# The first norm of a two-layer trunk: the input loaded a second time with tokens on partitions, and four of its products moved to GpSimd

## The chip, the cores and the metric

The kernel runs on one core of one Trainium2 chip. The metric is the device time of one execution in microseconds (us), the median of several runs. A core has five engines with instruction streams of their own: TensorE (PE, whose weight loads are PEld), VectorE (DVE), ScalarE (ACT), GpSimd (POOL) and SyncE (SP, which here only issues transfers). They wait for each other by semaphores. DMA engines move data between the chip's memory and the on-chip buffers. In the profile TensorE's clock is a share of full speed: 1.00 is the 2.4 GHz level, 0.50 the 1.2 GHz level.

## What is computed

The program is a trunk of two layers over 512 tokens of 1024 features, with 256 tokens of context beside them. The layer that the change touches begins with an RMSNorm, is modulated by a conditioning vector `c`, and goes into one wide projection:

```python
def rms_norm(x, w):
    x32 = x.astype(jnp.float32)
    y = x32 * lax.rsqrt(jnp.mean(x32 * x32, axis=-1, keepdims=True) + EPS)
    return (y * w.astype(jnp.float32)).astype(x.dtype)

def modulate(h, shift, scale):
    return h * (1.0 + scale) + shift
```

Shift and scale are products of the activated `c` with a modulation matrix, `ada_w`. The projected columns feed a bidirectional retention (queries, keys, values and a gate g) and a convolution. The retention's decay per head is a fixed function of the eight numbers `ret_decay_logit`. An output projection and a SwiGLU feed-forward follow, then a second layer of another kind.

## The kernel before, in words

Features lie on the 128 partitions. The residual stream is eight tiles `x0` to `x7`, one for each 128 features, of 128 x 512 (512 tokens). Every large product is done with both operands split into a high and a low part: three products (`mm3`, L506) of 128 x 128 by 128 x 512. The high part is a copy on ACT (`hi_of`), the low part a difference on DVE (`lo_of`). Nearly all records of an engine show the line of its helper: MM on PE is L328, DVE's helper is L299, ACT's L313, POOL's L307.

The work around the change is `even_start`. Its stages before the change:

- SP loads the eight tiles of xT (256 KB each), the constants kst, then the rows of `ada_w` (`load_ada`, two of 512 KB for each feature tile) and the rows of the projection's weights (`load_wr`, 512 KB per feature tile).
- ACT squares each tile of x, DVE adds the squares up, and PE multiplies the sum by a column of ones (`p4`), so that four columns of 128 tokens' sums stand on partitions. DVE makes `v` of them, and POOL raises it to the power of -1/2 (`r`). Four diagonal blocks of r (`dg`) times a matrix of ones give `pb`, the norm's factor of every token on all partitions.
- POOL has a chain of small operations before that power: a polynomial in `z` of 128 x 8 for the retention's decay. It ends in `lg`, `nlg`, `lw` and `xb`. All is issued in program order, and each engine works its stream off in order.
- `c_rows` spreads the activated conditioning rows over the partitions with two one-row matmuls for each of two rows (latents and context); ACT puts them into `cbx` and `cbc`. `dots(k, i)` takes the inner products of a tile's rows of `ada_w` with such a row on DVE (128 x 1024, with an accumulator), and `cols(k)` makes of them the columns `acol` and `xacc`.
- The loop over the eight feature tiles k: ACT takes the high parts of the weight rows, DVE runs `dots(k, 1)` and `cols(k)`, then t = x_k * rb (rb is pb copied by ACT), ACT applies scale and shift and takes the high part of t, DVE takes the low parts of the two weight halves, runs `dots(k + 1, 0)` and takes the low part of t. PE does 24 products per tile, into eight banks that stay open over all eight tiles.
- For k above 3 the weights of the queries are also loaded (`q_load`, L910 and L913), in four buffers shared with the weight rows. They are split by `q_split`, four times within the loop (`Q_AT`) and four times behind it: ACT takes the high part and its negative, and a transfer that POOL issues adds the weights to that negative, which leaves the low part (`add_dma`, L332, in the rows `a<-raw`). PE takes the query products up behind the loop. The line L476 in SP's rows loads the weights of g, which come next.

`warm()` issues products of ones that nothing reads. The name `pg` in the rows is any bank, `a` any 128 x 512 slot, `raw` a buffer of weight rows, `ar` one of rows of `ada_w`, `pw` (after the change) the bank of the warm products. What sets the order is the order of the code and, for transfers, the buffers that must be free.

Of the kernel before, what the change touches and what calls it, by code (L numbers as in the profile page):

```python
# [15 lines left out]
P = 128  # L16
D = 1024
# [27 lines left out]
WARM2 = 2  # L45
# [22 lines left out]
LATE_STEP = 2  # L68
COLD = 3.0
# [182 lines left out]
def trunk_kernel(ctx: ExitStack, tc: tile.TileContext, A, out: bass.AP):  # L252
# [94 lines left out]
    nc.scalar.dma_start(out=lgz, in_=A["ret_decay_logit"].partition_broadcast(P))  # L347
    ident = kst[:, K_ID:K_ID + P]
# [7 lines left out]
    ACT(out=first, in_=mhalf, func=AF.Exp)  # L356
    xT = []
    for k in range(KD):
        x = xres.tile([P, T], F32, name=f"x{k}")
        nc.sync.dma_start(out=x, in_=A["xT"][k * P:(k + 1) * P, :])  # L360
        xT.append(x)
    nc.sync.dma_start(out=kst, in_=A["kst"])
# [143 lines left out]
    def mm3(ps, L, R, first, last):  # L506
        (lh, ll), (rh, rl) = L, R
        MM(ps, lh, rl, start=first, stop=False)
        MM(ps, lh, rh, start=False, stop=False)
        MM(ps, ll, rh, start=False, stop=last)  # L510
        tick(3 * rh.shape[1] / 2400)
# [324 lines left out]
    def even_start(pool):  # L836
# [15 lines left out]

        crow = []
# [7 lines left out]
        def load_wr(k):  # L861
            wr = wraw.tile([P, D], F32, name=nm("raw"), tag="raw")
            nc.sync.dma_start(out=wr, in_=w_in[k * P:(k + 1) * P, 2048:3072])
            wrs.append(wr)
# [8 lines left out]
        def warm(n, rhs):  # L873

            ps = bank()
# [44 lines left out]

        raws.append(load_ada(0))
# [9 lines left out]
        sums = []  # L931
        for k in range(KD):
            q = slot()
            ACT(out=q, in_=xT[k], func=AF.Square)
            warm(WARM0, xT[k])
            if len(sums) == 2:
                TT(out=q, in0=sums.pop(0), in1=q, op=ALU.add)
            sums.append(q)
            if k == 0:
                e = pool.tile([P, 8], F32, name="z2")  # L940
                ACT(out=e, in_=z1, func=AF.Exp)
                ACT(out=first, in_=mhalf, func=AF.Silu)
                d2 = pool.tile([P, 8], F32, name="z3")
                GTS(out=d2, in0=e, scalar1=2.0, scalar2=None, op0=ALU.add)
                nc.vector.reciprocal(out=d2, in_=d2)
                sv = pool.tile([P, 8], F32, name="z4")
                GTT(out=sv, in0=e, in1=d2, op=ALU.mult)
                s2 = pool.tile([P, 8], F32, name="z5")
                GTT(out=s2, in0=sv, in1=sv, op=ALU.mult)
# [1174 lines left out]
```

## Time and profile before

| | |
|---|---|
| runs | 1117.42, 1117.03 and 1114.89 us, median 1117.03 us |
| profiled execution | 1115.2 us, of which the span of its engines' work is 1113.4 us |
| mean granted clock of TensorE | 0.991 |
| busy: PE, PEld | 1090.6 us (98%), 961.0 us (86%) |
| busy: DVE, ACT, POOL | 887.7 us (80%), 501.6 us (45%), 121.3 us (11%) |
| chain that ended last, by engine | PE 91%, DMA 2%, DVE 2%, issue 2%, POOL 1%, ACT 1% |

The times within the trace are microseconds from the start of the span. A row of a timeline gives the start, the time from the first start to the last end of neighbouring instructions of one form, the engine, the line, the operation, what it writes and reads, the shapes, the count, and in brackets how long the engine stood idle before and what ended that. SPq and POOLq are transfers being issued, and their landing is told in the DMA views.

### The profile page before, as it was taken

Reading aid. Unit: us, or ns where it says so; the run is one execution under the profiler, and the core shown is the slowest. Engines: PE = TensorE matmul, PEld = TensorE weight load, DVE = VectorE, ACT = ScalarE, POOL = GpSimd, SP = SyncE. Lnnn points to the kernel's source line nnn. Section 1 sums busy time; section 2 is a strip of 40 time slices with the busy share of each in tenths; the row PEclk is TensorE's granted clock in tenths of the full one; section 3 lists DMA queues with packets and bytes.
Section 4 is the critical chain, followed back from the end, with each engine's and each line's share of the span. In section 5 each row is a group of like instructions: output and inputs, shape, how many; then the busy total and the mean of one; then the engine's idle time right before and its main releaser. Section 6 shows DMA issues by size and latency. Waiting matters only on the chain.

```text
span 1113.4 us, 16976 instructions
## 1 busy us (share of the span) xinstructions
PE 1090.6 (98%) x6554; PEld 961.0 (86%) x6554; DVE 887.7 (80%) x1444; ACT 501.6 (45%) x759; POOL 121.3 (11%) x140
## 2 busy tenths in 40 slices
PE   6999999999999999999999999999999999999996
PEld 3878887469988999999999988899889999999996
DVE  5989998998779798788898788776796756667666
ACT  5556756567533344243345443534334442434331
POOL 4022122213000000000001010000001000000000
PEclk7999999999999999999999999999999999999998
DMA  9789976659266688777787335334755676565502
GB/s 352 235 217 263 279 190 162 176 178 232 87 209 196 175 250 244 221 205 225 210 243 196 124 114 189 114 77 137 208 147 139 149 178 161 144 168 136 148 11 76
DMA packets 132224, 199.42 MB, mean 179 GB/s; under 512 B 7088, under 2 KB 91440, under 8 KB 132144
## 3 DMA queue, kind: packets, MB, share of 16 engines
q1 hardware_dynamic: 99392, 137.01, 37.7%
q0 software_dynamic: 24592, 34.85, 19.1%
q10 hardware_dynamic: 8160, 26.48, 7.0%
q8 instruction: 51, 0.84, 0.3%
q14 instruction: 29, 0.24, 0.1%
HBM read 178.16 MB, written 2.10 MB: 162 GB/s over the span
## 4 chain that ended last, share of the span: by engine, by line
PE 91%; DMA 2%; DVE 2%; issue 2%; POOL 1%; ACT 1%; POOLq 0%; DVEq 0%; ACTq 0%
PE pg L328 61%; PE pg L1865 29%; PE pm L328 2%; DVE a L299 2%; DMA wl<-raw 1%; POOL z L307 1%; DMA a<-raw 1%; ACT a L313 1%; DMA x<-in_xT 0%; DMA raw<-in_ffn_w_gate 0%; ACT wh L313 0%; POOL s L307 0%; DVE wl L299 0%; DMA a<-a 0%; ACT dm L313 0%
## 5 line engine op out<-in xcount | busy, mean ns | idle before, releaser
L328 PE MATMUL pg<-a,wh 128*128 128x512 f32 (+1 forms) x1504 | 381.3, 344 | 1.0 <-DVE x L299 0.9
L313 ACT ACTIVATE wh<-raw 128x1024 fp32r<-128x1024 f32 (+1 forms) x219 | 227.2, 1042 | 324.4 <-PE pg L328 137.2
L1865 PE MATMUL pg<-a,wh 128*128 128x256 f32 x1792 | 323.4, 283 | 0.0
L299 DVE TENSOR_TENSOR wl<-raw,wh 128x1024 fp32r<-128x1024 f32 (+1 forms) x203 | 242.9, 1200 | 99.0 <-ACT wh L313 97.6
L328 PEld LDWEIGHTS pg<-a,wh 128*128 128x128 f32 x1504 | 260.4, 190 | 34.8 <-DVE x L299 1.3
L1865 PEld LDWEIGHTS pg<-a,wh 128*128 128x128 f32 x1792 | 281.0, 192 | 1.7
L328 PE MATMUL pg<-a,wl 128*128 128x512 f32 (+1 forms) x752 | 257.5, 343 | 0.0
L1865 PE MATMUL pg<-a,wl 128*128 128x256 f32 x896 | 253.6, 283 | 0.0
L1865 PEld LDWEIGHTS pg<-a,wl 128*128 128x128 f32 x896 | 172.0, 192 | 0.0
L328 PEld LDWEIGHTS pg<-a,wl 128*128 128x128 f32 x752 | 142.5, 190 | 16.8 <-issue 0.5
L328 PE MATMUL pg<-a,a 128*128 128x512 f32 (+2 forms) x572 | 128.1, 379 | 2.2 <-DMA a<-raw 1.5
L299 DVE SCALAR_TENSOR_TENSOR x<-pg,mod,x 128x512 f32<-128x512 f32 (+1 forms) x140 | 85.0, 625 | 47.8 <-PE pg L328 47.1
L328 PEld LDWEIGHTS pg<-a,a 128*128 128x128 f32 x572 | 97.3, 192 | 28.4 <-issue 8.8
L328 PE MATMUL pg<-gp,wh 128*128 128x512 f32 x384 | 118.6, 390 | 0.0
L299 DVE SCALAR_TENSOR_TENSOR ar<-ar,cbx 128x1024 f32<-128x1024 f32 (+1 forms) x70 | 81.7, 1172 | 8.8 <-DMA ar<-in_ada_wT 8.8
L299 DVE TENSOR_TENSOR a<-a,a 128x256 f32<-128x256 f32 (+3 forms) x142 | 75.4, 542 | 11.7 <-ACT a L313 9.1
L328 PEld LDWEIGHTS pg<-gp,wh 128*128 128x128 f32 x384 | 71.2, 188 | 14.2
L299 DVE SCALAR_TENSOR_TENSOR a<-a,vec,a 128x505 f32<-128x505 f32 (+14 forms) x115 | 78.5, 737 | 0.0
L328 PE MATMUL pg<-gp,wl 128*128 128x512 f32 x192 | 74.7, 389 | 0.0
L313 ACT ACTIVATE a<-pg 128x512 f32<-128x512 f32 (+2 forms) x79 | 41.3, 539 | 74.0 <-PE pg L328 38.9
L313 ACT ACTIVATE a<-a 128x512 fp32r<-128x512 f32 (+3 forms) x85 | 47.5, 570 | 53.0 <-DVE a L299 51.6
L299 DVE TENSOR_TENSOR a<-pg,a 128x512 f32<-128x512 f32 x80 | 54.6, 687 | 11.9 <-PE pg L1865 5.3
(134 smaller groups left out, 919.6 us busy)
## 6 DMA issues: line engine op xcount, KB each, us to landing
raw<-in_ffn_w_gate SPq DMA_DIRECT2D x52, 512.0 KB, 4.8
raw<-in_ffn_w_up SPq DMA_DIRECT2D x52, 512.0 KB, 4.8
ar<-in_ada_wT ACTq DMA_DIRECT2D x48, 512.0 KB, 5.0
raw<-in_ffn_w_down SPq DMA_DIRECT2D x40, 512.0 KB, 4.7
ar<-in_ada_wT SPq DMA_DIRECT2D x35, 512.0 KB, 6.1
raw<-in_even_w_in SPq DMA_DIRECT2D x24, 512.0 KB, 4.9
wl<-raw POOLq DMA_DIRECT2D x16, 512.0 KB, 6.6
raw<-in_ffn_w_gate POOLq DMA_DIRECT2D x16, 512.0 KB, 8.1
```

The source lines that it names most:

```text
L299: latest[0] = op(**kw).ins
L307: op(**kw)
L313: last_act[0] = nc.scalar.activation(**kw).ins
L328: nc.tensor.matmul(ps, L, R, start=start, stop=stop)
L1865: nc.tensor.matmul(o, x[:, s], y, start=fresh and p == k == j == 0, stop=False, skip_group_check=True)
```

## The change

`x` is handed to the kernel a second time in its other orientation and loaded first, as four tiles `xt` of 128 tokens x 1024 features (512 KB each), into slots that later hold rows of `ada_w`. The sums of squares are taken along a row: three by DVE's inner product (`row_dot`, 128 x 1024), the second one by ACT (Square with an accumulator). The squares of xT, DVE's additions and the product `p4` go. The tiles of xT are loaded inside `load_wr(k)`, one with each tile's weight rows, and kst goes to ACT's queue.

Both conditioning rows are spread before `pb`. Of the early warm products two stay, in a bank of their own, and three follow pb where there were two. `dots(0, 0)` and `dots(0, 1)` follow the diagonal blocks. In the first tile the weights' low parts and t's stand in another order, and `mm3` begins with the product of the two high parts (`high_first`). The multiplication t = x_k * rb of the second to fifth tile (`POOL_T`) is issued on GpSimd. The decay's polynomial with its exponential (`log_decay`) is issued behind the fifth tile's work (k = 4) instead of at the start.

```diff
--- before.py
+++ after.py
@@ -42,7 +42,7 @@
 DX_AT = (80.0, 84.0, 88.0, 92.0)
 ACT_SLOTS = 44
 WARM0 = 1
-WARM2 = 2
+WARM2 = 3
 HOLD = 3
 AR_BUFS = 3
 ADA_AHEAD = 6
@@ -66,6 +66,8 @@
 SIDE_EACH = 2
 SIDE_STEP = 3.5
 LATE_STEP = 2
+ACT_SQUARE = 1
+POOL_T = range(1, 5)
 COLD = 3.0
 SEVENS = (4, 4, 4, 4)
 GP_BUFS = 6
@@ -345,6 +347,7 @@
     kst = const.tile([P, K_N], F32, name="kst")
     lgz = const.tile([P, 8], F32, name="lgz")
     nc.scalar.dma_start(out=lgz, in_=A["ret_decay_logit"].partition_broadcast(P))
+    nc.scalar.dma_start(out=kst, in_=A["kst"])
     ident = kst[:, K_ID:K_ID + P]
     ones = const.tile([P, P], F32, name="ones")
     nc.vector.memset(ones, 1.0)
@@ -353,13 +356,10 @@
     eps = const.tile([P, 1], F32, name="eps")
     nc.vector.memset(eps, EPS)
     first = const.tile([P, 4], F32, name="first")
-    ACT(out=first, in_=mhalf, func=AF.Exp)
+    ACT(out=first, in_=mhalf, func=AF.Silu)
     xT = []
     for k in range(KD):
-        x = xres.tile([P, T], F32, name=f"x{k}")
-        nc.sync.dma_start(out=x, in_=A["xT"][k * P:(k + 1) * P, :])
-        xT.append(x)
-    nc.sync.dma_start(out=kst, in_=A["kst"])
+        xT.append(xres.tile([P, T], F32, name=f"x{k}"))
     cbx = const.tile([P, D], F32, name="cbx")
 
 
@@ -503,11 +503,11 @@
         low_part(lo[:, :cols], src, hi[:, :cols], name)
         return hi[:, :cols], lo[:, :cols]
 
-    def mm3(ps, L, R, first, last):
+    def mm3(ps, L, R, first, last, high_first=False):
         (lh, ll), (rh, rl) = L, R
-        MM(ps, lh, rl, start=first, stop=False)
-        MM(ps, lh, rh, start=False, stop=False)
-        MM(ps, ll, rh, start=False, stop=last)
+        three = [(lh, rh), (ll, rh), (lh, rl)] if high_first else [(lh, rl), (lh, rh), (ll, rh)]
+        for n, (x, y) in enumerate(three):
+            MM(ps, x, y, start=first and n == 0, stop=last and n == 2)
         tick(3 * rh.shape[1] / 2400)
 
     def cols_of(pair, i):
@@ -850,6 +850,7 @@
                 raws.append(raw)
             return raws
 
+        banks.update(g=list(range(7)), w=[7])
         crow = []
         for i in range(2):
             cr = pool.tile([P, D], F32, name=nm("ar"), tag="ar", bufs=START_BUFS)
@@ -859,6 +860,7 @@
         wrs = []
 
         def load_wr(k):
+            nc.sync.dma_start(out=xT[k], in_=A["xT"][k * P:(k + 1) * P, :])
             wr = wraw.tile([P, D], F32, name=nm("raw"), tag="raw")
             nc.sync.dma_start(out=wr, in_=w_in[k * P:(k + 1) * P, 2048:3072])
             wrs.append(wr)
@@ -872,7 +874,7 @@
 
         def warm(n, rhs):
 
-            ps = bank()
+            ps = bank("w")
             for _ in range(n):
                 MM(ps[:, :256], ones, rhs[:, :256], start=True, stop=True)
 
@@ -918,6 +920,12 @@
             n = len(Wq)
             Wq.append(split(q_raw[n // 2][:, n % 2 * T:(n % 2 + 1) * T], name='q'))
 
+
+        xt = []
+        for i in range(4):
+            x = whl.tile([P, D], F32, name=nm("xt"), tag=("wh", "wl")[i % 2])
+            nc.sync.dma_start(out=x, in_=A["x"][i * P:(i + 1) * P, :])
+            xt.append(x)
         raws.append(load_ada(0))
         nc.sync.dma_start(out=vec, in_=A["vec"])
         load_wr(0)
@@ -928,49 +936,42 @@
         TT(out=z1, in0=z1, in1=lgz, op=ALU.min)
         z0 = pool.tile([P, 8], F32, name="z0")
         TS(out=z0, in0=lgz, scalar1=0.0, scalar2=None, op0=ALU.min)
-        sums = []
-        for k in range(KD):
-            q = slot()
-            ACT(out=q, in_=xT[k], func=AF.Square)
-            warm(WARM0, xT[k])
-            if len(sums) == 2:
-                TT(out=q, in0=sums.pop(0), in1=q, op=ALU.add)
-            sums.append(q)
-            if k == 0:
-                e = pool.tile([P, 8], F32, name="z2")
-                ACT(out=e, in_=z1, func=AF.Exp)
-                ACT(out=first, in_=mhalf, func=AF.Silu)
...
-            if k == 4:
-                rows = list(c_rows(0, cbx))
-        for f in rows:
-            f()
-        TT(out=sums[1], in0=sums[0], in1=sums[1], op=ALU.add)
-        p4 = bank()
-        for j in range(4):
-            MM(p4[:, j:j + 1], sums[1][:, j * P:(j + 1) * P], ones[:, 0:1], start=True, stop=True)
-        dots(0, 0)
+        e = pool.tile([P, 8], F32, name="z2")
+        nlg = const.tile([P, 8], F32, name="nlg")
+
+        def log_decay():
+            d2 = pool.tile([P, 8], F32, name="z3")
+            GTS(out=d2, in0=e, scalar1=2.0, scalar2=None, op0=ALU.add)
+            nc.vector.reciprocal(out=d2, in_=d2)
...
+        ss = sm(4, "v")
+        for i in range(4):
+            if i < 2:
+                warm(WARM0, xt[i])
+            if i == ACT_SQUARE:
+                ACT(out=xt[i], in_=xt[i], func=AF.Square, accum_out=ss[:, i:i + 1])
+            else:
+                row_dot(xt[i], xt[i], ss[:, i:i + 1], last=False)
+            if i == 1:
+                for f in c_rows(0, cbx):
+                    f()
         v = sm(4, "v")
-        TS(out=v, in0=p4[:, :4], scalar1=1.0 / D, scalar2=EPS, op0=ALU.mult, op1=ALU.add)
+        TS(out=v, in0=ss, scalar1=1.0 / D, scalar2=EPS, op0=ALU.mult, op1=ALU.add)
         r = sm(4, "r")
         GTT(out=r, in0=v, in1=mhalf, op=ALU.pow)
         rows = list(c_rows(1, cbc))
-        dots(0, 1)
         dg = slot()
         for j in range(4):
             dj = dg[:, j * P:(j + 1) * P]
@@ -980,53 +981,58 @@
                 TS(out=dj, in0=ident, scalar1=r[:, j:j + 1], scalar2=None, op0=ALU.mult)
         pb = bank()
         MM(pb, ones, dg, start=True, stop=True)
-        warm(WARM2, xT[0])
+        dots(0, 0)
+        dots(0, 1)
+        warm(WARM2, xt[0])
         cols(0)
         rb = slot()
         banks["g"] = list(range(8))
         ps = [bank() for _ in range(8)]
         ps = ps[4:] + ps[:4]
+        raws.append(load_ada(1))
+        load_wr(1)
         for k in range(KD):
-            wh = [hi_of(wrs[k][:, :T]), hi_of(wrs[k][:, T:])]
-            if k:
-                dots(k, 1)
-                cols(k)
-            else:
-                W = [(wh[0], lo_of(wrs[k][:, :T], wh[0]))]
+            raw = [wrs[k][:, :T], wrs[k][:, T:]]
             t = slot()
             if k == 0:
                 STT(out=t, in0=xT[k], scalar=acol[:, k:k + 1], in1=pb, op0=ALU.mult, op1=ALU.mult)
+                wh = [hi_of(raw[0])]
                 th = slot(F32R)
                 ACT(out=th, in_=t, func=AF.Identity, bias=xacc[:, 0, k:k + 1])
+                ACT(out=rb, in_=pb, func=AF.Copy)
+                wh.append(hi_of(raw[1]))
+                W = [(wh[0], lo_of(raw[0], wh[0]))]
+                tl = slot(F32R)
+                STT(out=tl, in0=t, scalar=xacc[:, 0, k:k + 1], in1=th.bitcast(F32), op0=ALU.add, op1=ALU.subtract)
+                dots(k + 1, 0)
+                W.append((wh[1], lo_of(raw[1], wh[1])))
             else:
-                TT(out=t, in0=xT[k], in1=rb, op=ALU.mult)
+                wh = [hi_of(x) for x in raw]
+                dots(k, 1)
+                cols(k)
+                (nc.gpsimd.tensor_tensor if k in POOL_T else TT)(out=t, in0=xT[k], in1=rb, op=ALU.mult)
                 ACT(out=t, in_=t, func=AF.Identity, scale=acol[:, k:k + 1], bias=xacc[:, 0, k:k + 1])
                 th = hi_of(t)
-            if k:
-                W = [(wh[0], lo_of(wrs[k][:, :T], wh[0]))]
-            else:
-                ACT(out=rb, in_=pb, func=AF.Copy)
-            W.append((wh[1], lo_of(wrs[k][:, T:], wh[1])))
-            if k < KD - 1:
-                raws.append(load_ada(k + 1))
-                load_wr(k + 1)
-                if k:
+                W = [(h, lo_of(x, h)) for x, h in zip(raw, wh)]
+                if k == 1:
+                    tl = lo_of(t, th)
+                if k < KD - 1:
+                    raws.append(load_ada(k + 1))
+                    load_wr(k + 1)
                     dots(k + 1, 0)
-            if k == 0:
-                tl = slot(F32R)
-                STT(out=tl, in0=t, scalar=xacc[:, 0, k:k + 1], in1=th.bitcast(F32), op0=ALU.add, op1=ALU.subtract)
-                hx.append((th, tl))
-            else:
-                hx.append((th, lo_of(t, th)))
-            if k == 0:
-                dots(1, 0)
-            for i in (4, 5, 6, 7, 0, 1, 2, 3):
+                if k > 1:
+                    tl = lo_of(t, th)
+            hx.append((th, tl))
+            for i in (4, 5, 6, 7, 0, 1, 2, 3) if k else range(8):
                 hi, lo = W[i // 4]
                 s = slice((i % 4) * P, (i % 4 + 1) * P)
-                mm3(ps[i], (hi[:, s], lo[:, s]), hx[k], k == 0, k == KD - 1)
+                mm3(ps[i], (hi[:, s], lo[:, s]), hx[k], k == 0, k == KD - 1, True)
             if k == 0:
                 for f in rows:
                     f()
+            if k == 4:
+                ACT(out=e, in_=z1, func=AF.Exp)
+                log_decay()
             if k > 3:
                 q_load()
             for _ in range(Q_AT.count(k)):
@@ -2097,6 +2103,7 @@
     kst, lin, rope = shape_constants()
     arrays = {
         "xT": cont(f["x"][0].T),
+        "x": cont(f["x"][0]),
         "ctxT": cont(f["ctx"][0].T),
         "vec": cont(vec),
         "kst": kst, "lin": lin, "rope": rope,
```

The order of the instructions at three places, as the programs issue them. First POOL's stream from the norm's power to the first transfers that make the queries' low parts. `s` is the power, `z` to `xb` the decay's chain. Before:

```order
L307 TENSOR_TENSOR z_147<-z_147,z_143 128x8
L307 TENSOR_TENSOR lg<-z_131,z_147 128x8
L307 TENSOR_SCALAR nlg<-lg 128x8
L307 TENSOR_SCALAR lw<-lg,kst 128x4 x4
L307 TENSOR_SCALAR xb<-lg 128x4
L307 TENSOR_TENSOR s_216<-s_214,mhalf 128x4
L332 DMA a_542<-raw_488 128x512
L332 DMA a_598<-raw_488 128x512
```

The same stretch after the change. The rows left out are the chain's middle:

```order
L309 TENSOR_TENSOR s_153<-s_151,mhalf 128x4
L1013 TENSOR_TENSOR a_232<-x_90,a_174 128x512
L1013 TENSOR_TENSOR a_282<-x_91,a_174 128x512
L1013 TENSOR_TENSOR a_332<-x_92,a_174 128x512
L1013 TENSOR_TENSOR a_382<-x_93,a_174 128x512
L309 TENSOR_SCALAR z_433<-z_134 128x8
...
L309 TENSOR_TENSOR lg<-z_132,z_440 128x8
L309 TENSOR_SCALAR nlg<-lg 128x8
L309 TENSOR_SCALAR lw<-lg,kst 128x4 x4
L309 TENSOR_SCALAR xb<-lg 128x4
L334 DMA a_514<-raw_459 128x512
L334 DMA a_571<-raw_459 128x512
```

The power stands ahead of the chain now and four 128 x 512 multiplications behind it; the whole chain stands between these and the queries' transfers.

Next PE's stream ahead of the first real product. `x` and `xt` with `ones` are warm products, `ar` with `ones` the conditioning rows, `ones,a` of 128x1 is p4, and `a` with `ones` of 128x512 is pb. Before:

```order
L328 MATMUL pg_186<-ar_112,ones 128x512
L328 MATMUL pg_188<-ar_112,ones 128x512
L328 MATMUL pg_192<-x_98,ones 128x256
L328 MATMUL pg_197<-x_100,ones 128x256
L328 MATMUL pg_202<-x_102,ones 128x256
L328 MATMUL pg_208<-ones,a_200 128x1 x4
L328 MATMUL pg_218<-ar_114,ones 128x512
L328 MATMUL pg_220<-ar_114,ones 128x512
L328 MATMUL pg_228<-a_223,ones 128x512
L328 MATMUL pg_230<-x_88,ones 128x256 x2
L328 MATMUL pg_236<-a_263,a_246 128x512
```

After:

```order
L330 MATMUL pw_137<-xt_112,ones 128x256
L330 MATMUL pw_140<-xt_114,ones 128x256
L330 MATMUL pg_143<-ar_104,ones 128x512
L330 MATMUL pg_146<-ar_104,ones 128x512
L330 MATMUL pg_155<-ar_106,ones 128x512
L330 MATMUL pg_157<-ar_106,ones 128x512
L330 MATMUL pg_164<-a_159,ones 128x512
L330 MATMUL pw_168<-xt_112,ones 128x256 x3
L330 MATMUL pg_179<-a_194,a_192 128x512
```

Eight products of 128x256 with ones stood ahead of pb (the piece shows the last three of them), and p4; two products stand there now, and the four rows of the conditioning stay.

Last DVE's stream over the second feature tile, from its product t = x * rb or from its weights' low parts (`a<-raw,a`) to the columns of the third. Before:

```order
L299 TENSOR_TENSOR a_299<-x_90,a_235 128x512
L299 TENSOR_TENSOR a_304<-raw_261,a_292 128x512
L299 TENSOR_TENSOR a_306<-raw_261,a_294 128x512
L299 SCALAR_TENSOR_TENSOR dump,xacc<-ar_308,cbx 128x1024
L299 TENSOR_TENSOR a_315<-a_299,a_302 128x512
L299 SCALAR_TENSOR_TENSOR dump,xacc<-ar_310,cbx 128x1024
```

After:

```order
L301 SCALAR_TENSOR_TENSOR acol<-xacc,vec 128x1
L301 TENSOR_TENSOR a_244<-raw_188,a_233 128x512
L301 TENSOR_TENSOR a_246<-raw_188,a_235 128x512
L301 TENSOR_TENSOR a_248<-a_232,a_242 128x512
L301 SCALAR_TENSOR_TENSOR dump,xacc<-ar_250,cbx 128x1024
L301 SCALAR_TENSOR_TENSOR dump,xacc<-ar_252,cbx 128x1024
```

The first row is gone from DVE, and the low part of t stands ahead of both inner products instead of between them.

## Rows read from the trace of the kernel before

**Rows 1.** Page, part 1: busy time, share and count by engine.

```profile
PE 1090.6 (98%) x6554; PEld 961.0 (86%) x6554; DVE 887.7 (80%) x1444; ACT 501.6 (45%) x759; POOL 121.3 (11%) x140
```

**Rows 2.** Chain of waits, start to 62 us: start, duration, what.

```profile
0.73 3.86 DMA x<-in_xT
...
13.74 1.27 POOL z L307
...
17.59 1.02 POOL s L307
...
19.39 2.08 PE pg L328 x2
...
23.93 38.22 PE pg L328 x157
```

**Rows 3.** Chain of waits, 60 to 84 us.

```profile
69.47 7.93 DMA a<-raw
...
77.45 6.61 PE pg L328 x27
```

**Rows 4.** Windows: span, then PE, PEld, DVE, ACT, POOL, PEclk, DMA share, GB/s.

```profile
23.90:28.90 5.00, 4.97 (x12) 3.94 (x13) 4.90 (x10) 3.24 (x7) 0.00 (x0) 0.50 1.02 409
29.00:69.90 40.90, 40.90 (x181) 33.82 (x181) 37.69 (x74) 24.78 (x41) 4.01 (x5) 1.00 0.71 217
```

**Rows 5.** Timeline of PE up to the first real products.

```profile
4.72 4.28 PE L328 MATMUL pg<-x,ones 128*128 128x256 f32 x10 [4.72 <-DMA x<-in_xT]
8.93 1.98 PE L328 MATMUL pg<-ar,ones 1*128 1x512 f32 x4
10.84 1.56 PE L328 MATMUL pg<-x,ones 128*128 128x256 f32 x6
```

**Rows 6.** Timeline of ACT, the squares of x, the first high part.

```profile
6.82 3.73 ACT L313 ACTIVATE a<-x 128x512 f32<-128x512 f32 x7
22.27 0.72 ACT L313 ACTIVATE a<-a,xacc 128x512 fp32r<-128x512 f32 x1 [1.91 <-DVE a L299]
```

**Rows 7.** Timeline of DVE, the norm and the second to fourth tile.

```profile
13.64 0.16 DVE L299 TENSOR_SCALAR s<-pg 128x4 f32<-128x4 f32 x1
21.49 0.75 DVE L299 SCALAR_TENSOR_TENSOR a<-x,acol,pg 128x512 f32<-128x512 f32 x1 [0.92 <-PE pg L328]
33.40 1.22 DVE L299 SCALAR_TENSOR_TENSOR dump<-ar,cbx 128x1024 bf16<-128x1024 f32 x1
34.54 0.69 DVE L299 TENSOR_TENSOR a<-a,a 128x512 fp32r<-128x512 f32 x1
36.68 0.68 DVE L299 TENSOR_TENSOR a<-x,a 128x512 f32<-128x512 f32 x1
38.49 1.22 DVE L299 SCALAR_TENSOR_TENSOR dump<-ar,cbx 128x1024 bf16<-128x1024 f32 x1
```

**Rows 8.** Timeline of POOL: two operations of the chain.

```profile
9.46 0.49 POOL L307 TENSOR_TENSOR z<-z,z 128x8 f32<-128x8 f32 x1
15.40 0.20 POOL L307 TENSOR_TENSOR z<-z,z 128x8 f32<-128x8 f32 x1
```

**Rows 9.** Tile dm, POOL's operations: duration ns min/median/max, first and last start.

```profile
L307 POOL TENSOR_SCALAR dm<-lin,nlg x4: 365/840/1430, 95.9 to 200.1; 128x128 f32<-128x128 f32 x4
```

**Rows 10.** Timeline of DVE: beside the last of those, and behind it.

```profile
200.02 2.07 DVE L299 SCALAR_TENSOR_TENSOR a<-a,vec,a 128x503 f32<-128x503 f32 x3
202.61 1.38 DVE L299 SCALAR_TENSOR_TENSOR a<-a,vec,a 128x502 f32<-128x502 f32 x2
```

**Rows 11.** Timeline of POOL: the first of the queries' transfers issued.

```profile
50.56 0.97 POOL L332 DMA_DIRECT2D a<-raw  x1 [31.96 <-DVE a L299]
```

**Rows 12.** Waits of SP's queue, 50 to 84 us: total, times, longest.

```profile
SPq L913 <- DMA a<-raw: 5.1, 1, 5.1
```

**Rows 13.** DMA issues, 50 to 60.6 us: count, KB each, us to landing.

```profile
raw<-in_even_w_in SPq DMA_DIRECT2D x3, 512.0 KB, 3.9
a<-raw POOLq DMA_DIRECT2D x3, 256.0 KB, 3.7
```

More of the change, by code (lines that the diff above doesn't have):

```diff
@@ L930, in even_start @@
         TS(out=z0, in0=lgz, scalar1=0.0, scalar2=None, op0=ALU.min)
-        sums = []
-        for k in range(KD):
-            q = slot()
-            ACT(out=q, in_=xT[k], func=AF.Square)
-            warm(WARM0, xT[k])
-            if len(sums) == 2:
-                TT(out=q, in0=sums.pop(0), in1=q, op=ALU.add)
-            sums.append(q)
-            if k == 0:
-                e = pool.tile([P, 8], F32, name="z2")
-                ACT(out=e, in_=z1, func=AF.Exp)
-                ACT(out=first, in_=mhalf, func=AF.Silu)
[L943 to L949, printed above, removed]
-                pl = pool.tile([P, 8], F32, name="z6")
-                GTS(out=pl, in0=s2, scalar1=-2.0 / 17, scalar2=-2.0 / 15, op0=ALU.mult, op1=ALU.add)
-                for n in (13, 11, 9, 7, 5, 3, 1):
-                    GTT(out=pl, in0=pl, in1=s2, op=ALU.mult)
-                    GTS(out=pl, in0=pl, scalar1=-2.0 / n, scalar2=None, op0=ALU.add)
-                GTT(out=pl, in0=pl, in1=sv, op=ALU.mult)
-                GTT(out=lg, in0=z0, in1=pl, op=ALU.add)
-                nlg = const.tile([P, 8], F32, name="nlg")
-                GTS(out=nlg, in0=lg, scalar1=-1.0, scalar2=None, op0=ALU.mult)
-            if k == 4:
-                rows = list(c_rows(0, cbx))
@@ L961, in even_start @@
-        for f in rows:
-            f()
-        TT(out=sums[1], in0=sums[0], in1=sums[1], op=ALU.add)
-        p4 = bank()
-        for j in range(4):
-            MM(p4[:, j:j + 1], sums[1][:, j * P:(j + 1) * P], ones[:, 0:1], start=True, stop=True)
-        dots(0, 0)
+        e = pool.tile([P, 8], F32, name="z2")
[4 more added lines that the diff above has]
+            nc.vector.reciprocal(out=d2, in_=d2)
+            sv = pool.tile([P, 8], F32, name="z4")
+            GTT(out=sv, in0=e, in1=d2, op=ALU.mult)
+            s2 = pool.tile([P, 8], F32, name="z5")
+            GTT(out=s2, in0=sv, in1=sv, op=ALU.mult)
+            pl = pool.tile([P, 8], F32, name="z6")
+            GTS(out=pl, in0=s2, scalar1=-2.0 / 17, scalar2=-2.0 / 15, op0=ALU.mult, op1=ALU.add)
+            for n in (13, 11, 9, 7, 5, 3, 1):
+                GTT(out=pl, in0=pl, in1=s2, op=ALU.mult)
+                GTS(out=pl, in0=pl, scalar1=-2.0 / n, scalar2=None, op0=ALU.add)
+            GTT(out=pl, in0=pl, in1=sv, op=ALU.mult)
+            GTT(out=lg, in0=z0, in1=pl, op=ALU.add)
+            GTS(out=nlg, in0=lg, scalar1=-1.0, scalar2=None, op0=ALU.mult)
```

## The prediction

> **What bounds the kernel.** I read the busy shares first: PE is busy for 98% of the span [rows 1]. A change can win only where PE waits or runs slowly: at the start, and where a stage's input comes late. The chain of waits shows the start [rows 2]: x lands, POOL works off its small operations, its power `s` at 17.59 makes pb (two matmuls from 19.39), and PE is on the chain from 23.93. The chain of the next stage shows the one wait behind it, a queries' transfer at 69.47 [rows 3].
>
> The windows then say what sets the pace [rows 4]. Up to 28.9 the clock is 0.50, the 1.2 GHz level, and twelve products take 5 us (0.42 each). From 29.0 it is 1.00 and 181 take 40.9 us (0.227, so 5.44 for a tile of 24). DVE needs 5.09 per tile (33.40 to 38.49 [rows 7]). PE is therefore the slower one at full clock, but in the first three tiles it feeds on what DVE has ready. I call E the time at which the eight tiles are done: 69.9 before. E less six tiles is 37.26, where PE took up the third tile; its low part was ready at 34.54 + 0.69 = 35.23 [rows 7]. So before, DVE was 2.0 ahead there, thanks to the slow clock.
>
> **Start of the loop.** The chain's stay ahead of the power goes. What is late next? x in its new form lands at the old rate: the last square ends at 6.82 + 3.73 = 10.55 [rows 6], so 2 MB is in at about 10. One inner product of 1.22 [rows 7], v (0.16, which stood at 13.64 [rows 7]) and the power of 1.02 [rows 2] end at 12.8, and the diagonal blocks at 13.5. That would be 5 us earlier. But PE's own queue takes that place: two warm products and four conditioning rows stand ahead of pb. Each is two records. The warm records took 0.43 at first (ten in 4.28) and 0.26 later (six in 1.56), the conditioning records 0.5 at the later pace (four in 1.98) [rows 5]. From this I take PE at the slow pace until it has worked some us without a break, here with the first tile landing at 4.6 + 0.6 = 5.2 (twice the bytes of the old first one [rows 2], at 409 GB/s [rows 4]) and the second at 6.5: two products of two records to 7.3, eight conditioning records of 1.0 to 15.3. This is the new wait, 1.8 us for pb. Queued behind it are the warm products and the first real products, which need pb anyway. At the faster pace from 9 on it would be about 1 us less; I keep the slow one. pb takes 2.08 [rows 2], to 17.3. From the start of t to the first high part was 22.27 + 0.72 - 21.49 = 1.50 [rows 6, 7], so that stands at 18.8, before at 23.0: 4.2 earlier.
>
> **From there to the third tile.** Before, the third tile's low part followed the first high part by 35.23 - 22.99 = 12.2. Now two multiplications of t (0.68 less overlap, 0.6 each [rows 7]) leave DVE, the first tile's second low part of the weights (0.6) moves behind the high part, and ACT makes DVE wait about 0.45 in the new order: within 0.2 of the same, 12.2. So it is ready at 31.0. PE, started 4 us earlier at the slow clock, has worked two tiles off by about then and waits for DVE; the lead of 2.0 is gone. E = 31.0 + 0.14 + 6 x 5.44 = 63.8: 6.1 earlier, without a price for GpSimd.
>
> **GpSimd's four multiplications.** What 128 x 512 with two inputs costs there, and costs DVE beside it, no row shows. The nearest is its 128 x 128 operation with one input: 0.365 alone, 1.43 beside three DVE products [rows 9]. Those three took 2.07, the same two behind it 1.38 [rows 10]: 0.69 each, at most 0.035 more in one. From below I take 0.035 for 128 columns of one input, so 8 x 0.035 = 0.28 per tile, which it may just as well keep hidden. From above, DVE stands for as long as GpSimd works: alone (0.365 - 0.20) [rows 8, 9] for 128 columns, 1.3 for 1024 input columns, about 1.4 with its start. The measured row is near the lower end but is of another form; I take 0.5. They depend on nothing but x_k and rb, so three of them run ahead of the third tile's low part: 1.5. E is 65.3, 4.6 earlier.
>
> A rule of the Trainium skill bears on this ("SBUF — State Buffer", section "Who interferes with whom"): GpSimd shares its port pair with a second one of DVE and the pair is locked for one of them exclusively. By it the upper end holds where a two-input DVE operation meets one of GpSimd; the measured 0.035 beside two-input products speaks against a hold for a whole instruction. Its figure for an fp32 tensor_tensor of 2048 ("GPSIMD Engine Reference", section "3.1 Elementwise — side-by-side cycle accounting") is 4497 ns against 2293 on DVE, 1.96 times; an estimate by that is 0.68 x 1.96 = 1.33 us for each of the four, near the upper end, as in rival B.
>
> **The decay's chain, now ahead of the queries.** It stands in POOL's stream between the four multiplications and the first queries' transfer. Before, that transfer was issued at 50.56 [rows 11], E - 19.3, long after the chain. Now the chain starts behind the reciprocal in the fifth tile, about E - 23. An operation alone took 0.20, beside DVE 0.49 [rows 8] and 1.27 beside an inner product [rows 2]: one per DVE operation. DVE does seven or eight per tile of 5.09, 25 operations are 3.6 tiles, some faster ones at the end: the chain ends at about E - 3.3. Four transfers follow at once (0.97 each to issue [rows 11], 3.7 to land [rows 13]): E + 0.2 to E + 4. PE wants the first low part at E + 0.5 and the fourth at E + 4.6, so these do. But the buffers come free with them: the fourth load of the queries' weights, which before waited 5.1 for such a transfer [rows 12], goes out when the second has landed, E + 1.4 instead of E - 10.4, lands 3.9 later [rows 13], is split on ACT (two copies, about 1.3 as the 0.72 of rows 6), and the seventh transfer goes out at E + 6.6. It lands 3.7 [rows 13] to 7.93 [rows 3] later, at E + 10.3 to E + 14.5. PE takes six products for each low part, 1.36, so it wants the seventh at E + 8.7: late by 1.6 to 5.8. Before, the transfer of rows 3 landed at 77.40, E + 7.5, where the fifth was wanted at E + 5.9: late by 1.6, which is now given back. From 0 to +4.2; I take +2.5, as the rope and context loads, which go over the same engines as that slow transfer, still stand there.
>
> The sum against the profiled execution (1115.2: a span of 1113.4 and 1.8 around it): -4.6 + 2.5 = -2.1, so 1113.1. The runs' median of 1117.03 stands 1.8 above that execution.
>
> **Edits at no cost.** Each tile now brings 1.75 MB instead of 1.5: at 409 GB/s [rows 4] 4.3 us, within PE's 5.44; without that cover the tile is late by what passes 5.44. The switch to the exponential's table now falls into the loop, in ACT's waits, which are long: 24.78 busy of 40.9 [rows 4]; uncovered it would cost its own length once. `p4`, the squares and the sums go from engines that waited; nothing behind them is bound by it but the start counted above. `high_first` lets a tile's first product start with the high part alone; after the first tile DVE's low part is the bound and it gives nothing.
>
> **Rivals.**
> - A, the best case: GpSimd costs DVE 0.28 per tile (0.84 in all) and the queries' pass is no later than before: -6.1 + 0.8 = -5.3, 1109.9. For it: the measured 0.035. Against it: the chain moved 16 us later, with transfers that already waited.
> - B, GpSimd holds DVE for its whole instruction: 4 x 1.4 = 5.6 instead of 1.5, +4.1 on the forecast: 1117.2. For it: GpSimd's own durations double beside DVE [rows 8]. Against it: DVE's hardly move [rows 10].
> - C, slower: the chain's pace. At 1.1 or more per operation (as 1.27 beside the inner products [rows 2], 1.43 [rows 9]) it ends at E + 4.2 instead of E - 3.3, all queries' low parts are late by that, and the pass with them: +7.5, 1120.6. It decides from a chain that ends later than about E + 3, where it alone eats the whole gain. Against it: 0.49 beside DVE's additions [rows 8], and seven or eight of DVE's operations in 5.09 us leave no more than 0.7 for one on the mean.
>
> **Chances.** Forecast 0.42 (its own range 1110.7 to 1115.0), A 0.25, B 0.18, C 0.15. The range reaches from below A to between B and C: 1108.6 to 1119.0, with most of C and the far end of A outside. 0.2% (2.2 us) is about what the runs can tell from no change. Faster than that against the median: A, and most of the forecast's case, 0.61. No change: a part of the forecast and most of B, 0.20. Slower: C and the rest of B, 0.19.
>
> **What the changed profile would show.** The start: PE without a break from about 5.2 to pb, which ends near 17.3, and the first real product near 19; if pb starts before 14.5 the conditioning rows cost less. GpSimd's L1013 rows: four of 1.3 to 2.5 us each; DVE's neighbours longer by tenths (forecast), by nothing (A) or by more than a us (B). The pace: 24 products every 5.44 from the third tile, first with a wait for DVE. The chain's `xb` a few us ahead of E (forecast), behind it (C), or much earlier (A). The queries' pass: a wait for `a<-raw` of some us near its seventh low part. The forecast is wrong if E moves by less than 2 us, or if the pass behind E takes over 17 us.

## The result, and the profile after

The changed kernel takes 1125.80 us (median of 4, 1125.50 to 1126.22), the kernel before 1116.39 in the same comparison: a ratio of 1.0085 (95% interval 1.0069 to 1.0101). I had forecast 1113.1. The profiled execution took 1125.5 with a span of 1123.7, 10.3 more than before.

E, the end of the eight tiles, is at 68.8 instead of 69.9. The queries' pass behind it, 48 products, lasts until 93.8 instead of 82.8: 25.0 instead of 12.8 us. (In PE's timeline below E is the start of the 143rd product of the row at 36.43, and the pass ends where the 11th of the row at 89.34 starts.) So the stretch up to E gave 1.2, the pass cost 12.2, and the rest of the program gave back 0.7. The chain of waits of the changed kernel shows the pass (the counterpart of [rows 2, 3]; start, duration, what):

```profile
45.61 0.27 POOL z L309
...
60.04 0.76 POOL lw L309
...
61.89 4.86 POOL lw L309 x3
...
66.84 0.06 POOL xb L309
...
67.70 4.39 DMA a<-raw
...
72.24 7.93 DMA raw<-in_even_w_in
...
81.77 7.52 DMA a<-raw
...
89.34 10.77 PE pg L330 x37
```

The reader is to see four things in a row: GpSimd's decay chain runs from 45.61 to 67; only then do the queries' transfers go out; the last weights' load starts when one of them has landed (72.2) and takes 7.93; and the seventh transfer, which needs that load, takes 7.52. PE goes on at 89.34. PE's timeline of the changed kernel, the counterpart of [rows 5]:

```profile
6.43 1.19 PE L330 MATMUL pw<-xt,ones 128*128 128x256 f32 x2 [6.43 <-DMA xt<-in_x]
...
9.13 7.19 PE L330 MATMUL pg<-ar,ones 1*128 1x512 f32 x8
16.25 2.08 PE L330 MATMUL pg<-a,ones 128*128 128x512 f32 x2
...
20.41 6.56 PE L330 MATMUL pg<-a,a 128*128 128x512 f32 x24
...
36.43 32.93 PE L330 MATMUL pg<-a,a 128*128 128x512 f32 x144 [1.24 <-DVE a L301]
...
89.34 11.00 PE L330 MATMUL pg<-a,a 128*128 128x512 f32 x38 [7.74 <-DMA a<-raw]
```

Products start at 20.41 (before 23.93 [rows 2]). But in the third tile PE does two products and then waits for DVE until 36.43, hardly before the 37.26 at which the kernel before took that tile up. Its windows show the clock over the wait of 7.74 (columns as [rows 4]):

```profile
80.00:89.00 9.00, 1.60 (x6) 0.91 (x6) 0.02 (x2) 2.41 (x4) 1.74 (x2) 0.70 1.06 333
89.00:94.00 5.00, 4.66 (x11) 3.71 (x12) 0.04 (x1) 1.18 (x2) 0.00 (x0) 0.52 0.62 169
```

While PE stood, the clock fell; in the 5 us behind it is 0.52, near the 1.2 GHz level, and eleven products take 4.66, 0.42 each. At 0.227 they would take 2.5: about 2.2 us of the loss are that.

ACT's row of the first high part is the counterpart of [rows 6], DVE's timeline that of [rows 7], and the GpSimd products beside it stand below:

```profile
19.15 0.72 ACT L315 ACTIVATE a<-a,xacc 128x512 fp32r<-128x512 f32 x1 [3.06 <-DVE a L301]
```

```profile
20.57 2.31 DVE L301 SCALAR_TENSOR_TENSOR dump<-ar,cbx 128x1024 bf16<-128x1024 f32 x1
...
23.42 2.31 DVE L301 SCALAR_TENSOR_TENSOR dump<-ar,cbx 128x1024 bf16<-128x1024 f32 x1
...
28.34 2.31 DVE L301 SCALAR_TENSOR_TENSOR dump<-ar,cbx 128x1024 bf16<-128x1024 f32 x1
...
32.24 2.39 DVE L301 TENSOR_TENSOR a<-raw,a 128x512 fp32r<-128x512 f32 x2
...
35.70 0.68 DVE L301 TENSOR_TENSOR a<-a,a 128x512 fp32r<-128x512 f32 x1
```

```profile
20.43 1.36 POOL L1013 TENSOR_TENSOR a<-x,a 128x512 f32<-128x512 f32 x1 [7.17 <-ACT a L315]
23.25 1.40 POOL L1013 TENSOR_TENSOR a<-x,a 128x512 f32<-128x512 f32 x1 [1.46 <-DMA x<-in_xT]
27.77 1.80 POOL L1013 TENSOR_TENSOR a<-x,a 128x512 f32<-128x512 f32 x1 [3.12 <-DMA x<-in_xT]
32.28 1.80 POOL L1013 TENSOR_TENSOR a<-x,a 128x512 f32<-128x512 f32 x1 [2.71 <-DMA x<-in_xT]
```

Each product lies beside one DVE row, and that row is 1.1 us longer than its like: 2.31 instead of 1.22 [rows 7], 2.39 for two instead of 1.29 (tt_dve, below).

### The profile page after: what moved, and what is told of

It reads as the page before. It is cut to its first block, busy times and chain, and to the rows that moved or that the text cites. A ratio compares the mean times of both kernels' runs of the same rounds, so it can differ in the third digit from the quotient of the medians.

```text
span 1123.7 us, 16936 instructions
## 1 busy us (share of the span) xinstructions
PE 1093.2 (97%) x6536; PEld 959.0 (85%) x6536; DVE 889.1 (79%) x1439; ACT 498.9 (44%) x752; POOL 136.8 (12%) x144
## 4 chain that ended last, share of the span: by engine, by line
PE 88%; DMA 5%; DVE 2%; POOL 2%; issue 2%; ACT 1%; SPq 0%; POOLq 0%; DVEq 0%; ACTq 0%
PE pg L330 57%; PE pg L1871 29%; DMA raw<-in_even_w_in 2%; DVE a L301 2%; PE pm L330 2%; POOL z L309 1%; DMA a<-raw 1%; DMA xt<-in_x 1%; POOL lw L309 1%; ACT a L315 0%; DMA ar<-in_ada_wT 0%; DMA raw<-in_ffn_w_gate 0%; DVE wl L301 0%; DMA a<-a 0%; POOL s L309 0%
## 5 line engine op out<-in xcount | busy, mean ns | idle before, releaser
L330 PE MATMUL pg<-a,a 128*128 128x512 f32 (+2 forms) x572 | 131.7, 383 | 12.5 <-DMA a<-raw 10.0
L330 PEld LDWEIGHTS pg<-gp,wh 128*128 128x128 f32 x384 | 71.2, 188 | 14.1
L301 DVE TENSOR_TENSOR a<-a,a 128x256 f32<-128x256 f32 (+3 forms) x135 | 71.2, 536 | 9.7 <-ACT a L315 7.1
```

The source lines that it names most:

```text
L301: latest[0] = op(**kw).ins
L330: nc.tensor.matmul(ps, L, R, start=start, stop=stop)
```

## The experiments

E and the pass behind it are read from each trace as above. One thing said ahead needs a reservation: the order of the code need not be the only thing that sets the order, as the build may place an instruction elsewhere. No run here shows that. Where an experiment moves the decay's chain behind the power or the last product, it is tied to that instruction (`issue_after`), so that its place is certain.

**tt_dve: the products back on DVE.**

```diff
-POOL_T = range(1, 5)
+POOL_T = ()
```

> The changed kernel with the four products t = x * rb back on DVE, all else as changed. Theory (each GpSimd product holds DVE for 1.1 us, as the neighbours at 20.57, 23.42, 28.34 and 32.24 show): the third tile's low part comes 4 x 1.1 - 2 x 0.6 = 3.2 us earlier, E = 65.6 instead of 68.8, the queries' pass as long as in the changed kernel: 1125.8 - 3.2 = 1122.6 us. Rival (those long DVE rows come from the full DMA engines, 405 GB/s there): they stay 2.3 us long, and DVE has two products more: 1126 to 1127 us.

Measured: 1123.96 us, ratio 1.0075 (1.0057 to 1.0093). DVE's rows in its timeline, at the same DMA load:

```profile
20.71 1.22 DVE L301 SCALAR_TENSOR_TENSOR dump<-ar,cbx 128x1024 bf16<-128x1024 f32 x1
...
30.24 1.29 DVE L301 TENSOR_TENSOR a<-raw,a 128x512 fp32r<-128x512 f32 x2
...
32.59 0.69 DVE L301 TENSOR_TENSOR a<-a,a 128x512 fp32r<-128x512 f32 x1
```

The long rows are gone with the DMA engines as full as before (406 GB/s from 20.4 to 33.3 in both kernels), the third tile's low part is ready at 33.28 instead of 36.38, and E is 65.7: 3.1 earlier, as expected. The median fell by 1.8 only, since the pass became longer by 1.1 (26.1); the intervals of the two ratios overlap, so it is E that shows the effect and not the time. The rival that blamed the full DMA engines falls.

**early_exp: the decay's chain starts behind the last product, at 33.5.**

```diff
-    ACT(out=first, in_=mhalf, func=AF.Silu)
+    ACT(out=first, in_=mhalf, func=AF.Exp)
...
+        ACT(out=e, in_=z1, func=AF.Exp)
+        ACT(out=first, in_=mhalf, func=AF.Silu)
+        d2 = pool.tile([P, 8], F32, name="z3")
+        GTS(out=d2, in0=e, scalar1=2.0, scalar2=None, op0=ALU.add)
+        nc.vector.reciprocal(out=d2, in_=d2)
...
+                    last_t = nc.gpsimd.tensor_tensor(out=t, in0=xT[k], in1=rb, op=ALU.mult).ins
...
             if k == 4:
-                ACT(out=e, in_=z1, func=AF.Exp)
-                log_decay()
+                with tc.issue_after(last_t):
+                    log_decay()
```

> The changed kernel with the exponential and the reciprocal of the decay at the start, so that the decay's chain can start on GpSimd at once behind the fourth product (at about 34 instead of 45.6). Theory (the chain ahead of the queries' transfers makes the pass late): it ends at about 55, the transfers go out from there, and the pass behind E takes 13 to 14.5 instead of 24.8 us: 1125.8 - 10.5 = 1115.3 us. Rival (the pass is late because x and weights of the loop are loaded later and fill the DMA engines): no change, 1124.5 to 1126 us.

Measured: 1114.97 us, ratio 0.9990 (0.9980 to 1.0000). Its GpSimd timeline, and PE's row in the pass:

```profile
48.27 5.08 POOL L309 TENSOR_SCALAR lw<-lg,kst 128x4 f32<-128x4 f32 x4
53.43 0.52 POOL L309 TENSOR_SCALAR xb<-lg 128x4 f32<-128x4 f32 x1
53.90 0.97 POOL L334 DMA_DIRECT2D a<-raw  x1
```

```profile
76.23 17.28 PE L330 MATMUL pg<-a,a 128*128 128x512 f32 x70 [1.23 <-DMA a<-raw]
```

The first transfer goes out at 53.9 instead of 67.0, E is where it was (68.9), the pass takes 13.5, and 10.8 us come back. The chain's place is the main loss. The edit also takes one load of ACT's table (1.28 us at 44.01 in the changed kernel) out of the loop; since E stayed, that load had cost the tiles nothing that E shows.

**tt_dve_chain_start: both GpSimd edits undone.** `POOL_T = ()`, the exponential at the start as in early_exp, and `log_decay()` directly behind the power instead of at k = 4:

```diff
-        GTT(out=r, in0=v, in1=mhalf, op=ALU.pow)
+        power = nc.gpsimd.tensor_tensor(out=r, in0=v, in1=mhalf, op=ALU.pow).ins
+        with tc.issue_after(power):
+            log_decay()
```

> The changed kernel with the four products on DVE and the decay's chain directly behind the norm's power on GpSimd: what is left of the change is x with tokens on partitions, the order of the start and the first tile. Theory (the two GpSimd edits are the whole loss): E at 65.6 and a pass of about 13 us: 1125.8 - 3.2 - 12 = 1110.6 us. Rival (loading xT by tiles, 1.75 MB each, makes the tiles late): above 1114 us.

Measured: 1111.33 us, ratio 0.9956 (0.9940 to 0.9973). E 66.5, pass 13.7, and the rival (above 1114) falls. In this profiled execution x landed 1.0 later (first use at 7.32 instead of 6.27 in tt_dve), which is most of what E is above 65.6.

**b_pow_first: the kernel before, with only the chain behind the power.** The same tie, in the kernel before.

> The kernel before with one change: the decay's chain stands behind the norm's power on GpSimd instead of ahead of it. Theory (the start of before waited for GpSimd alone): the power starts at 13.8 instead of 17.56, the first high part 3.7 earlier, E 2 to 5.5 earlier (the lead of 2.0 that DVE had goes first): 1111 to 1114.5 us. Rival (PE at the slow clock takes the whole gain): 1115.5 to 1116.4 us.

Measured: 1113.22 us, ratio 0.9979 (0.9965 to 0.9994). E 67.4, 2.5 earlier, pass 13.3. The power starts at 14.26 but takes 1.96, its first part beside an inner product of DVE:

```profile
14.26 1.96 POOL L958 TENSOR_TENSOR s<-s,mhalf 128x4 f32<-128x4 f32 x1 [8.11 <-DVE s L299]
```

The queue's order alone is worth about half of what tt_dve_chain_start gains with the new loads as well: 0.21 of 0.44%, and both intervals are wide.

**b_chain_k4: the kernel before, with only the chain moved to k = 4.** The block of exponential, reciprocal and chain stands in the loop behind the fifth tile's products. The power no longer waits for it, as in b_pow_first.

> The kernel before with the one part of the change that I hold for the main loss: the decay's exponential and chain are issued behind the fifth tile (k = 4), all else as before. Theory (the two sides of that move are separate): the start gains what the kernel b_pow_first gained, E about 67.4, and the queries' pass takes about 25 us behind E as in the changed kernel instead of 12.85: 1116.1 - 2.5 + 12 = 1125.6 us. Rival (the pass is late only where xT's loads and GpSimd's products are in the loop as well): below 1119 us.

Measured: 1128.86 us (1124.01 to 1129.97), ratio 1.0108 (1.0084 to 1.0132). E is 66.1, the pass 25.2, and its chain of waits is that of the changed kernel, `raw` 7.99 and then `a<-raw` 7.30:

```profile
69.79 7.99 DMA raw<-in_even_w_in
...
79.45 7.30 DMA a<-raw
...
86.80 13.30 PE pg L328 x47
```

So neither xT's loads nor GpSimd's products are needed for the loss, and the rival (below 1119) falls. The profiled execution, 1124.0, fits the 1125.6 worked out; the median is 3.3 above it. Why the unprofiled runs took 4 to 6 us more than the profiled one stays open.

**q3_own: a buffer of its own for the queries' last load.**

```diff
-            wr = wraw.tile([P, 1024], F32, name=nm("raw"), tag="raw")
+            if len(q_raw) == 3:
+                wr = pool.tile([P, 1024], F32, name="rawq")
+            else:
+                wr = wraw.tile([P, 1024], F32, name=nm("raw"), tag="raw")
```

> The changed kernel with one buffer more: the last load of the queries' weights has its own and doesn't wait for a transfer to land. Theory (the 24.8 us behind E come from that load, which goes out at 72.2 only, lands 7.9 later and is then split, and from the seventh transfer behind it): its data are there by about 60, the seventh and eighth transfer go out right behind the six at about 73 and land by 80, the pass takes about 16: 1116 to 1118 us. Rival (the transfers that go out as a bundle at 67 are the loss, whatever the load does): above 1122 us.

Measured: 1117.57 us, ratio 1.0011 (1.0001 to 1.0020); the pass 16.8 instead of 25.0. PE's timeline has short waits now and no long one:

```profile
80.01 1.66 PE L330 MATMUL pg<-a,a 128*128 128x512 f32 x6 [0.44 <-DMA a<-raw]
82.00 1.65 PE L330 MATMUL pg<-a,a 128*128 128x512 f32 x6 [0.33 <-DMA a<-rawq]
84.42 11.85 PE L330 MATMUL pg<-a,a 128*128 128x512 f32 x51 [0.77 <-DMA a<-rawq]
```

Of the 12.2 the wait for that buffer, with the clock that falls behind it, makes 8.2. The other 4.0 are the pace at which the eight transfers land: from 70.3 to 84.4 (the eighth was expected by 80), one in 2.0 us, where PE works off a low part in 1.36. The first three, landing by 73.4, came 1.5 to 1.6 apart, the others 1.8 to 2.6, with the loads behind them in flight from 72.0 on; how much of the pace is the bundle itself and how much those loads, no run separates.

**b_tt_pool: the kernel before, with only the products on GpSimd.**

```diff
-                TT(out=t, in0=xT[k], in1=rb, op=ALU.mult)
+                (nc.gpsimd.tensor_tensor if 1 <= k <= 4 else TT)(out=t, in0=xT[k], in1=rb, op=ALU.mult)
```

> The kernel before with one change: the products t = x * rb of the second to fifth tile on GpSimd. There x lies in the buffers by about 10 and the DMA engines are as full as before. Theory (each such product holds the DVE operation beside it for 1.1 us): all four run from about 23.5 on, ahead of the third tile's low part, which comes 4 x 1.1 - 2 x 0.6 = 3.2 later at 38.4; DVE's lead of 2.0 hides the first part of that, E = 71.2 instead of 69.9: 1117.0 to 1118 us. Rival (the loss came with the loads of x inside the loop): DVE has two products less, 1115 to 1116.5 us, no DVE row of 128x1024 above 1.3 us.

Measured: 1117.10 us, ratio 1.0002 (0.9992 to 1.0013). The time is inside what was expected, the way there only in part. The four products run from 23.70 to 30.75, and DVE's timeline beside them is:

```profile
23.85 2.32 DVE L299 SCALAR_TENSOR_TENSOR dump<-ar,cbx 128x1024 bf16<-128x1024 f32 x1
...
26.20 2.19 DVE L299 SCALAR_TENSOR_TENSOR dump<-ar,cbx 128x1024 bf16<-128x1024 f32 x1
...
28.43 1.12 DVE L299 TENSOR_TENSOR xacc<-xacc,vec 128x2 f32<-128x2 f32 x1
29.59 1.18 DVE L299 SCALAR_TENSOR_TENSOR acol<-xacc,vec 128x1 f32<-128x1 f32 x1
```

Even a DVE operation of 128 x 1 takes 1.18 instead of 0.16: it stands until GpSimd is done. The third tile's low part came at 38.2, as worked out. But PE waited 4.0 for the second tile and ran its first products behind that wait slowly (24 in 7 us), so E went to 73.6 instead of 71.2. The pass shrank from 12.8 to 10.9. Its last four transfers went out 3.7 later, as E did, but the loads of rope and context kept their times within 0.8, and the four landed in 4.5 us in the median. In the kernel before, beside those loads, they took 8.3:

```profile
a<-raw POOLq DMA_DIRECT2D x4, 256.0 KB, 8.3
```

So 2.0 of the 3.7 came back in the pass. That the loads' company made the difference is read from these times; no run moves them alone.

**probe: the price by form and size.** The products are on DVE; GpSimd works at their places for nothing that is read.

```diff
+                if 1 <= k <= 4:
+                    probe = slot()
+                    n = (512, 128, 256, 512)[k - 1]
+                    if k == 1:
+                        nc.gpsimd.tensor_scalar(out=probe[:, :n], in0=xT[k][:, :n], scalar1=2.0, scalar2=None, op0=ALU.mult)
+                    else:
+                        nc.gpsimd.tensor_tensor(out=probe[:, :n], in0=xT[k][:, :n], in1=rb[:, :n], op=ALU.mult)
+                TT(out=t, in0=xT[k], in1=rb, op=ALU.mult)
```

> The changed kernel with the four products on DVE, and with four more GpSimd operations at the places where the products stood, whose output nothing reads: in the second tile a tensor_scalar of 128x512 with one input, then tensor_tensor of 128x128, 128x256 and 128x512 with two. Only DVE's rows beside them are read. Theory (a two-input operation holds DVE for as long as it works): the neighbours are longer by 0.3, 0.6 and 1.1, the one beside the tensor_scalar by under 0.1, as the row of 0.035 that I took. Rival (any GpSimd operation of that size holds DVE): that one is longer by 0.5 or more. Other rival (a fixed price per operation): 1.1 at all sizes.

GpSimd's four operations, and then the DVE rows beside them:

```profile
18.70 1.51 POOL L1017 TENSOR_SCALAR a<-x 128x512 f32<-128x512 f32 x1 [5.49 <-DMA x<-in_xT]
23.26 0.57 POOL L1019 TENSOR_TENSOR a<-x,a 128x128 f32<-128x128 f32 x1 [3.05 <-DMA x<-in_xT]
27.71 0.91 POOL L1019 TENSOR_TENSOR a<-x,a 128x256 f32<-128x256 f32 x1 [3.89 <-DMA x<-in_xT]
32.23 1.93 POOL L1019 TENSOR_TENSOR a<-x,a 128x512 f32<-128x512 f32 x1 [3.61 <-DMA x<-in_xT]
```

```profile
19.00 0.86 DVE L301 TENSOR_TENSOR a<-raw,a 128x512 fp32r<-128x512 f32 x1
...
23.55 0.30 DVE L301 TENSOR_TENSOR xacc<-xacc,vec 128x2 f32<-128x2 f32 x1
...
28.06 1.64 DVE L301 SCALAR_TENSOR_TENSOR dump<-ar,cbx 128x1024 bf16<-128x1024 f32 x1
...
32.97 1.74 DVE L301 TENSOR_TENSOR a<-a,a 128x512 fp32r<-128x512 f32 x1
```

Without such a neighbour these DVE rows take 0.68, 0.16, 1.22 and 0.69. So DVE loses 0.14 beside two inputs of 128 columns, 0.42 at 256 and 1.05 at 512, and 0.18 beside one input of 512. The price grows with the size, and the second input makes most of it; each is one operation in one execution. The one-input price is above the 0.1 that I expected, those at 128 and 256 columns are below the 0.3 and 0.6. The DVE row beside the 128 columns met only the last part of that operation.

**best1: the second conditioning row behind pb, on top of tt_dve_chain_start.**

```diff
-        rows = list(c_rows(1, cbc))
...
         MM(pb, ones, dg, start=True, stop=True)
+        rows = list(c_rows(1, cbc))
```

> The kernel tt_dve_chain_start with the second conditioning row (c_rows(1)) behind pb on PE instead of ahead of it. Theory (PE's own queue, not the norm, sets pb): pb starts about 2.2 earlier, the third tile's low part as well, but PE, which does the row's four records behind pb instead, starts the products no earlier and is then the bound at the slow clock: 0.5 to 1.5 us better, 1110.3 us. Rival (pb waits for x and the power, not for PE): no change, 1111.0 to 1111.6 us.

Measured: 1110.23 us, ratio 0.9943 (0.9928 to 0.9958).

```profile
14.05 2.08 PE L330 MATMUL pg<-a,ones 128*128 128x512 f32 x2 [1.26 <-ACT a L315]
```

pb starts at 14.05 instead of 17.20, and waits 1.26 for ACT's part of the diagonal; so PE's own queue had held it. The products start no earlier (22.13 instead of 21.35) and E is 66.6. The interval overlaps that of tt_dve_chain_start (0.9940 to 0.9973): a gain over it is not shown.

**best2 and best2_own: best1 without the last warm products, and that with the buffer of q3_own.**

```diff
-WARM2 = 3
+WARM2 = 0
```

> The kernel best1 without the warm products behind pb and the second conditioning row (WARM2 = 0): six records, 19.77 to 22.7 in best1. Theory (PE is the bound of the first two tiles there, the third tile's low part being ready at 31.4 and taken up at 33.98): products start at about 19.9, E 1.5 earlier at 65.1: 1108.7 us. Rival (they bring the clock's rise forward): products start earlier but run at 0.43 for longer, no change: 1109.8 to 1110.6 us.

> The kernel best2 with the extra buffer for the last load of the queries' weights (as in q3_own). Theory: where the transfers go out in the loop again, the pass has only one wait of about 1 us left (0.97 at 72.3 in best1), and the buffer isn't its cause: 0 to 1 us better than best2, 1107.7 to 1108.7 us. Rival (the load's earlier landing crowds others): slower than best2 by up to 1 us.

Measured: 1110.29 us, ratio 0.9953 (0.9936 to 0.9969), and 1111.45, 0.9960 (0.9945 to 0.9975). In best2 products start at 20.53 and E is 65.8, 0.8 earlier than in best1; its 24 products of the first tile take 7.0 instead of 6.2 (first start to last). The times of the two kernels overlap, and no gain is shown. With the transfers in the loop no gain of the extra buffer is shown either. Best1 and best2 beat the kernel before by 0.5 to 0.6%.

## Why the prediction was wrong

- **The start** was right in kind and 1.1 short. The power came at 12.23 and PE's conditioning rows did keep pb until 16.25, the new wait that I named; the first high part was ready at 19.87, not 18.8. The tiles of x were used at 6.43 and 8.01, not at 5.2 and 6.5, so the conditioning rows began 1.8 later; they took 7.2 instead of 8.0. I had counted one transfer's bytes, and four were issued one behind the other; whether that is the cause no run shows.
- **To the third tile, and GpSimd's products.** The step that failed is "The measured row is near the lower end but is of another form; I take 0.5". It was wrong in the size, 1.1 instead of 0.5, and in the count: all four products ran ahead of the third tile's low part, where I had three. Four at 1.1 are 4.4, not 1.5. The low part came at 36.38, 16.5 behind the first high part instead of 12.2, and PE went on at 36.43 with six tiles less the two products that it had done: 36.4 + 32.6 - 0.5 = 68.5, measured 68.8. So the step from the low part to E held. The row of 0.035 had one input and 128 columns; even 512 columns of one input cost only 0.18 in the probe. Two inputs and 512 columns hold DVE until GpSimd is done, in each DVE form that stood beside them here, down to 128 x 1. All of these forms have two inputs themselves; what a one-input form of DVE would lose no run shows. That is rival B's mechanism, at 1.1 instead of 1.4. The Trainium skill ("SBUF — State Buffer", section "Who interferes with whom") calls the shared port pair an exclusive lock; the runs agree for the two-input form (1.05 to 1.1 us of a 1.36 to 1.93 us operation). For the one-input form they do not: DVE's product at 19.00 in the probe lost 0.18, though GpSimd worked until 20.21.
- **The decay's chain** is the step that turned the sign: "+2.5" for the queries' pass was +12.2. Its operations took 21.3 us, and it ended at E - 1.9, near the forecast's E - 3.3, so rival C's condition (E + 3) was not met, and yet the loss was larger than C's. What failed is "goes out when the second has landed, E + 1.4 ..., lands 3.9 later". Six transfers left GpSimd as one bundle, the second landed at E + 3.3, the load issued behind it took 7.93 beside them, and the seventh transfer 7.52. I had taken one transfer's quiet duration [rows 13] for a time at which six of them, the next weights, rope and context all came at once, though [rows 3] showed 7.93 for that company. So the seventh low part came at E + 20.5, not at E + 14.5 at the latest. Then the clock fell over the long wait, 2.2 us, a term that I had not at all. early_exp and b_chain_k4 show the chain's place as the cause from both sides, q3_own the buffer as two thirds of it.
- **The signs and the sums.** Both signs of being wrong that I had named came: E moved by 1.2, less than 2, and the pass took over 17. Two slips in the working changed nothing: GpSimd's upper price comes out of its own rows as 1.32 + 0.20 = 1.5 and not 1.4, and the chain's end at E - 3.3 needs PE's 5.44 for a tile, not the 5.09 given.
- **Rival A** falls with both prices. That the loads of x by tiles were hidden holds: tt_dve took the third tile up on DVE's time, with no wait for a landing.

What stays open: how the other 4 us of the pass split between the bundle of transfers and the loads behind it, what the first tiles of x waited for, and why b_chain_k4's unprofiled runs were slower than its profiled one.

## What to carry to other kernels

A long chain of small operations on a queue is not priced by when it ends but by what it holds back: follow the transfers behind it to the buffers they free, and to the loads that wait for these, and price those loads at the busiest moment they can fall into. A product moved off a busy engine is no relief if the engine that takes it holds the first one up, here for 1.1 us where it saved 0.6; look for the price in the same form and size, and if there is none, the upper end is the honest one to put in the sum. And before an input is loaded twice to shorten a start, look at what stands ahead of the critical instruction in its queue: that order alone gave 0.2% here.

## What the runs showed of the hardware that was not expected

- A GpSimd tensor_tensor of 128x512 made a two-input DVE operation of 128x1 beside it last 1.18 us instead of 0.16; a tensor_scalar of the same size cost its two-input DVE neighbour 0.18.
- GpSimd's `lw` operations of 128x4 took 1.6 us each beside DVE's 128x1024 products (three in 4.86), where they took 0.27 at the start of the kernel before (four in 1.10).
- Transfers that add 256 KB landed in 3.3 to 3.8 us with little beside them and in 7.9 to 8.5 beside the loads of rope and context (kernel before); as a bundle of eight they landed one in 2.0 us (q3_own).
- After 7.7 us without work on PE the granted clock was 0.52 over the next 5 us.
